# Extra rows multiplied four weight blocks at a time, their activation behind the two halves, and other steps for slots and turns in a mixture-of-experts block

## The chip, the cores and the metric

The kernel runs on one core of a Trainium2 chip, as one program. The metric is the device time of one execution in microseconds (us), the median of several runs. Besides the times there is one profiled execution, with the start and the duration of each engine's instructions and DMA packets.

## The reference

A block of an encoder over 1024 tokens of width 1024: a layer norm, two mixers (RWKV-7 and forgetting attention), an output projection, a layer norm, an expert layer with the top 4 of 32 experts, and a last layer norm. The change lies in the expert layer and in the last norm.

```
def _moe(h, router_w, router_b, w1, b1, w2, b2):
    logits = (xt @ router_w + router_b).astype(jnp.float32)
    top_val, top_idx = lax.top_k(logits, TOP_K)
    gates = jax.nn.softmax(top_val, axis=-1)
    ...
    def expert_block(args):
        xb, e = args
        hid = xb @ w1[e] + b1[e]
        x_glu = jnp.minimum(hid[..., ::2], SWIGLU_LIMIT)
        x_lin = jnp.clip(hid[..., 1::2], -SWIGLU_LIMIT, SWIGLU_LIMIT)
        act = x_glu * jax.nn.sigmoid(SWIGLU_ALPHA * x_glu) * (x_lin + 1)
        return act @ w2[e] + b2[e]
    ...
h = _layer_norm(x, ln_in_w, ln_in_b)
...
h = _layer_norm(DEEPNORM_ALPHA * h + mix, ln1_w[l], ln1_b[l])
ffn = _moe(h, ...)
h = _layer_norm(DEEPNORM_ALPHA * h + ffn, ln2_w[l], ln2_b[l])
```

## The kernel before

The first 1036 us (norms, mixers, projection, routing) are the same program in both kernels. Then the 32 experts run one after the other, in the order of the list `SEQ`, each with 128 rows ("main" rows); the 18 fullest ones have 32 rows more (the extras). In the order of the program the experts 4 to 28 form five periods of five: extras, extras, none, extras, none. So in each period one expert with extras follows another: 4 and 5, 9 and 10, 14 and 15, 19 and 20, 24 and 25. Expert 31, the last, has none.

**Weights.** An expert has twelve weight blocks of 1 MB, eight for `up` and four for `down`. SP loads each into one of six buffers `raw` (L1178). ScalarE rounds it to `wh` (the cast, L1185), VectorE takes the rest, `wl = raw - wh` (L1188). Both have four buffers, so a cast waits until TensorE has finished the block four places back. `weights(j, ahead)` calls these three blocks ahead of TensorE.

**Matmuls.** A block's main rows take twelve matmuls of 512 columns (xh with wh, xh with wl, xl with wh): in `up` into the PSUM tile `h` (L1213), in `down` into `o` (L1271). The extras are multiplied in fp32 straight from `raw`, into a PSUM tile `ex` of which there is one buffer, shared by `up` (L1206) and `down` (L1261). Their stationary side is 32 wide, and the trace has eight of them for a block. TensorE runs up(0), up(1), down(0), up(2), down(1) and so on: `down(r-1)` follows `up(r)`.

**Activation.** `act` gives the pieces of the swiglu (L1223 to L1227): `extra` reads `ex` of `up(r)` and writes `lx` (on VectorE gx, lx, lx, lx, with a sigmoid sx on ScalarE); `half(0)` and `half(1)` read two banks each of `h` and write `lm`. The `turns` transpose `lm` (tile `tr`, L1150), round it to `ah` on ScalarE (L1152) and take `al` on VectorE (L1153); the last turn transposes `lx` to `ax` (L1248). The bank `tr` has one buffer too.

**Steps.** Jobs run after each block: step 0 to 7 after the blocks of `up(r)`, 8 to 11 after those of `down(r-1)`. `plan(r, where, f)` puts a job there; XP and TP hold the steps of the pieces of the next expert's inputs and of the turns, SLP that of the slots. The slots work finds the rows of a coming expert: small matmuls (L1014, L1020), a copy `st` and `sv` to `gate` on VectorE (L1029, L1004 to L1010), and, for one with extras, a second small matmul from `st` (L1026). Each engine runs its own instructions in the order of the program.

After expert 31 its turns and the transposes of the one-hot matrix (L1401) come, then `down(31)`, then `final_norm`: eight sums of 128 tokens on TensorE (L1466, L1469), the statistics on VectorE, an inverse root by Newton steps in `chain` (L1478 to L1487), which `advance` runs one step at a time between other work, and scaling on ScalarE (L1496), GpSimd (L1497) and VectorE.

Of the kernel before, what the change touches and what calls it, by code (L numbers as in the profile page):

```python
# [18 lines left out]
P = 128  # L19
# [25 lines left out]
XP = (4, 5, 7)  # L45
TP = (11, 13, 14)
SLP = -4
# [7 lines left out]
XB = 2  # L55
# [1058 lines left out]
def experts(tc, A, L):  # L1114
# [3 lines left out]
    with ExitStack() as cx:  # L1118
# [55 lines left out]
        def weights(j, ahead):  # L1174

            while len(raws) < min(j + src[1], len(stream)):
                raw = wr.tile([P, 2 * FF], FT, name="raw", tag=src[0], bufs=src[2])
                sp.dma_start(raw, stream[len(raws)]())  # L1178
                raws.append(raw)
            while len(ready) < min(j + 1 + ahead, len(stream)):  # L1180
                i = len(ready)
                raw = raws[i]
                if i == len(highs):
                    highs.append(wr.tile([P, 2 * FF], FR, name="wh", bufs=WB))
                    ac.copy(highs[i], raw)  # L1185
                h = highs[i]
                l = wp.tile([P, 2 * FF], FR, name="wl", bufs=WB)
                ve.tensor_tensor(l, raw, f32(h), op=OP.subtract)  # L1188
                ready.append((raw, h, l))
            return ready[j]  # L1190

        def up(j0, sel, xh, xl, xt, step=lambda s: None):
# [6 lines left out]
            def extra(k, raw):  # L1199
                if px is None:  # L1200
                    return
# [6 lines left out]
            late = []  # L1208
            for k in range(KD):
                raw, h, l = weights(j0 + k, AH[xt is not None] if src[0] == "raw" else 0)  # L1210
                for x, w, z in ((xh, h, False), (xh, l, False), (xl, h, k == KD - 1)):
                    for c, m in enumerate(cols):
                        pe.matmul(ps[:, c], x[:, k], w[:, m], start=False, stop=z)  # L1213
                late.append((k, raw))
                if len(late) == XB:
                    for b in late:
                        extra(*b)
                    late.clear()
                step(k)
# [9 lines left out]
        def act(ps, px):  # L1229
# [20 lines left out]
            return [extra, lambda: half(0), lambda: half(1)], turns + [piece], (ah, al, ax)  # L1250

        def down(j0, ah, al, ax, gate, idx, step=lambda s: None, o=None):
# [3 lines left out]
            def extra(b, raw):  # L1256
                for c in range(2 if px is not None else 0):
# [5 lines left out]
            late = []  # L1263
            for b in range(4):
                raw, h, l = weights(j0 + b, AH[ax is not None] if src[0] == "raw" else 0)
# [6 lines left out]
                late.append((b, raw))  # L1272
                if len(late) == XB:
                    for x in late:
                        extra(*x)
                    late.clear()
# [62 lines left out]

        at = {}  # L1340
# [7 lines left out]
        with tc.manual_schedule():  # L1348
# [11 lines left out]
            for r in range(NE):  # L1360
# [18 lines left out]
                run_all(parts[:-2])  # L1379
                for i in range(2):  # L1380
                    jobs.setdefault(12 * r + DP + i, []).insert(0, parts[i - 2])
                for w, f in zip(TP, turns):
# [11 lines left out]

            ring = lambda: wr.tile([P, 2 * FF], FT, name="raw", bufs=RB)
            kept = ring()
            oht = kept[:, :S].rearrange("p (t q) -> p t q", t=NT)
            for g in range(2):
                ps = pq.tile([P, 4, P], FT, name="tr")
                for j in range(4):  # L1400
                    pe.matmul(ps[:, j], last_oh[0][:, 4 * g + j], idb, start=True, stop=True)  # L1401
                ac.copy(oht[:, 4 * g:4 * g + 4], ps)
# [8 lines left out]
            sums()  # L1411
            down(at["d", NE - 1], *prev, o=kept[:, S:])
# [37 lines left out]
def final_norm(tc, A, L, ep, pt, wb, ys, oht, o):  # L1450
# [51 lines left out]
    def advance(to_end=False):  # L1502
        nonlocal run
        while run is not None:
# [3 lines left out]
            if not to_end:  # L1508
                return

    for g0, g1 in zip(FG, FG[1:]):
# [9 lines left out]
        advance(True)  # L1521
# [5 lines left out]
    advance(True)  # L1527
# [58 lines left out]
```

## Time and profile before

| | |
|---|---|
| runs | 2580.55, 2583.0, 2586.46 us; median 2583.0 |
| profiled execution | 2580.89 us, of which its span 2579.2 |
| busy share of the span | TensorE 93%, VectorE 75%, ScalarE 51%, GpSimd 16% |
| before the experts | 0 to 1035.6 us |
| experts | 1035.6 to about 2530 us |
| final norm | 2531.8 to 2579.2 us |

Busy times are shares over a stretch; matmul records overlap, so that the distance of two starts says what a matmul costs. In brackets stands how long an engine sat idle before an instruction, and what ended it.

### The profile page before, as it was taken

To read this page: it belongs to the slowest core of one execution; us is meant where nothing else is said; L and a number is where in the kernel's file an instruction comes from. 1 tells how busy PE (TensorE), PEld (TensorE's weight loads), DVE (VectorE), ACT (ScalarE), POOL (GpSimd) and SP (SyncE) were. 2 spreads that over 40 slices of the span, in tenths; PEclk is the share of its full clock that TensorE was granted. 3 is DMA by queue.
4 is the path that set the end of the run, shared out by engine and by line. 5 is a ranking of instruction groups with operands and counts; after the bars stand their busy time and mean duration, and the time that the engine had idled before them with its cause. 6 is when DMAs were issued, how large, how long until landed. Compare 5 with 4: busy or idle time off the path is not lost. (4 is left out here: it accounts for less than half of the span.)

```text
span 2579.2 us, 37473 instructions
## 1 busy us (share of the span) xinstructions
PE 2399.2 (93%) x14105; PEld 1808.3 (70%) x14105; DVE 1928.0 (75%) x2886; ACT 1321.3 (51%) x1610; POOL 400.6 (16%) x370
## 2 busy tenths in 40 slices
PE   5999998989988996899999999999999999999986
PEld 5778998977776674657666666766676666667663
DVE  8367334376887687779788888888888888888884
ACT  3254432354344432456666656666565655666661
POOL 4400211123122011011101011011110110111012
PEclk9999999999999997899999999999999999999998
DMA  6323864228446424768878778888877897788973
GB/s 228 130 74 136 284 203 86 69 70 259 158 150 242 138 83 180 258 206 308 299 301 322 274 294 301 311 292 322 297 282 284 312 330 282 277 298 306 344 279 136
DMA packets 184442, 606.63 MB, mean 235 GB/s; under 512 B 69881, under 2 KB 95609, under 8 KB 130626
## 3 DMA queue, kind: packets, MB, share of 16 engines
q1 hardware_dynamic: 155810, 525.24, 55.0%
q0 software_dynamic: 17456, 65.02, 8.9%
q10 hardware_dynamic: 10992, 13.93, 1.8%
q8 instruction: 113, 1.85, 0.3%
q14 instruction: 71, 0.58, 0.1%
HBM read 518.64 MB, written 85.50 MB: 234 GB/s over the span
## 5 line engine op out<-in xcount | busy, mean ns | idle before, releaser
L1188 DVE TENSOR_TENSOR wl<-raw,wh 128x2048 fp32r<-128x2048 f32 x384 | 873.8, 2289 | 195.2 <-ACT wh L1185 194.1
L1185 ACT CAST wh<-raw 128x2048 fp32r<-128x2048 f32 x381 | 720.6, 1906 | 110.6 <-DMA raw<-w 83.4
L1213 PE MATMUL h<-wh,xh 128*128 128x512 f32 x1024 | 299.6, 414 | 0.9 <-ACT wh L1185 0.9
L1213 PE MATMUL h<-wl,xh 128*128 128x512 f32 x1024 | 281.3, 396 | 1.1 <-DVE wl L1188 1.1
L1213 PE MATMUL h<-wh,xl 128*128 128x512 f32 x1024 | 280.3, 395 | 0.0
L1213 PEld LDWEIGHTS h<-wl,xh 128*128 128x128 f32 x1024 | 193.2, 189 | 48.2 <-DVE wl L1188 1.6
L1213 PEld LDWEIGHTS h<-wh,xl 128*128 128x128 f32 x1024 | 192.4, 188 | 46.6
L1213 PEld LDWEIGHTS h<-wh,xh 128*128 128x128 f32 x1024 | 184.3, 190 | 52.9 <-ACT wh L1185 10.6
L1009 POOL DMA_INDIRECT xg<-h_d,idx x32 | 71.6, 2239 | 924.0 <-PE slots L1026 469.5
L153 PE MATMUL mm<-whi,hT_lo 128*128 128x256 f32 x640 | 187.1, 293 | 10.9 <-DVE hT_lo L182 7.3
L151 PE MATMUL mm<-whi,hT_hi 128*128 128x256 f32 x640 | 187.4, 294 | 6.0 <-ACT sq L476 4.3
L152 PE MATMUL mm<-wlo,hT_hi 128*128 128x256 f32 x640 | 186.1, 292 | 0.0
L1271 PE MATMUL o<-wh,ah 128*128 128x512 f32 x512 | 173.3, 420 | 0.0
L1271 PE MATMUL o<-wl,ah 128*128 128x512 f32 x512 | 164.9, 404 | 0.0
L1271 PE MATMUL o<-wh,al 128*128 128x512 f32 x512 | 164.0, 402 | 0.0
L1224 ACT ACTIVATE sm<-gm 128x512 f32<-128x512 f32 x64 | 40.4, 632 | 211.9 <-DVE gm L1223 211.9
L1206 PE MATMUL ex<-raw,xt 128*32 128x512 f32 x1152 | 139.7, 603 | 0.0
L153 PEld LDWEIGHTS mm<-whi,hT_lo 128*128 128x128 f32 x640 | 126.9, 199 | 12.9 <-DVE hT_lo L182 8.5
L151 PEld LDWEIGHTS mm<-whi,hT_hi 128*128 128x128 f32 x640 | 126.9, 198 | 9.3 <-ACT sq L476 4.7
L152 PEld LDWEIGHTS mm<-wlo,hT_hi 128*128 128x128 f32 x640 | 126.9, 198 | 0.0
L1271 PEld LDWEIGHTS o<-wh,ah 128*128 128x128 f32 x512 | 92.1, 193 | 34.8 <-issue 15.1
L1271 PEld LDWEIGHTS o<-wl,ah 128*128 128x128 f32 x512 | 98.8, 193 | 24.1
(432 smaller groups left out, 4177.7 us busy)
## 6 DMA issues: line engine op xcount, KB each, us to landing
raw<-w SPq DMA_DIRECT2D x384, 1024.0 KB
pks<-pk_d SPq DMA_DIRECT2D x16, 1152.0 KB
pk_d<-pk POOLq DMA_DIRECT2D x16, 896.0 KB, 5.6
h_d<-h SPq DMA_DIRECT2D x17, 512.0 KB
raw<-w_fx ACTq DMA_DIRECT2D x8, 1024.0 KB
fx_d<-fraw POOLq DMA_DIRECT2D x64, 128.0 KB, 2.6
qkvo<-fx_d SPq DMA_DIRECT2D x32, 256.0 KB
x<-x SPq DMA_DIRECT2D x8, 512.0 KB
```

The costliest lines, as they stand in the source:

```text
L151: pe.matmul(ps, hi[:, k, n], whi[:, k], start=(k == 0), stop=False)
L152: pe.matmul(ps, hi[:, k, n], wlo[:, k], start=False, stop=False)
L153: pe.matmul(ps, lo[:, k, n], whi[:, k], start=False, stop=(k == KD - 1))
L1009: gp.indirect_dma_start(out=x, out_offset=None, in_=h1_d, in_offset=bass.IndirectOffsetOnAxis(ap=idx[0:m, i:i + 1], axis=0))
L1185: ac.copy(highs[i], raw)
L1188: ve.tensor_tensor(l, raw, f32(h), op=OP.subtract)
L1206: pe.matmul(px[32 * c:32 * c + 32], xt[:, k], raw[:, m], start=False, stop=(k == KD - 1))
L1213: pe.matmul(ps[:, c], x[:, k], w[:, m], start=False, stop=z)
L1224: ac.activation(sg, g, AF.Sigmoid, scale=SWI)
L1271: pe.matmul(po[:, c], x[:, k], w[:, m], start=(k == 0 and x is ah and w is h), stop=z)
```

## The change

- The extras of `up` are multiplied after block 1 (for the blocks 0 to 3) and block 5 (4 to 7); before, after blocks 1, 3, 5 and 7 for two blocks each. In `down` all four come after block 1; before, after 1 and 3.
- `act` hands out its pieces as half(0), half(1), extra. `half(0)` runs at step 8 and `half(1)` at step 9 as before; `extra`, which ran ahead of step 8, is now planned for step 9 (DP + 1) and stands there behind `half(1)`.
- The slots move from step 8 to step 7, an expert's third input piece from step 7 to 6, the turn of `lx` from step 14 to 15 (after block 3 of the next `up`).
- Expert 31's halves run at once, its turns at steps 10 and 11, and the one-hot transposes at steps 8 and 9, all within `down(30)`.
- `advance()` in the final norm runs two steps of the chain a call.

```
-XP = (4, 5, 7)
-TP = (11, 13, 14)
-SLP = -4
+XP = (4, 5, 6)
+TP = (11, 13, 15)
+SLP = -5
...
-XB = 2
+XB = 4
+XM = 1
...
-                late.append((k, raw))
-                if len(late) == XB:
-                    for b in late:
-                        extra(*b)
-                    late.clear()
+                if px is not None and k % XB == XM:
+                    for b in range(k - XM, k - XM + XB):
+                        extra(b)
                 step(k)
...
-            return [extra, lambda: half(0), lambda: half(1)], turns + [piece], (ah, al, ax)
+            return [lambda: half(0), lambda: half(1), extra], turns + [piece], (ah, al, ax)
...
+                if px is not None and b == XM:
+                    for x in range(XB):
+                        extra(x)
                 step(KD + b)
...
                 parts, turns, a = act(*hid)
-                run_all(parts[:-2])
-                for i in range(2):
-                    jobs.setdefault(12 * r + DP + i, []).insert(0, parts[i - 2])
-                for w, f in zip(TP, turns):
+                if r < NE - 1:
+                    for i in range(2):
+                        jobs.setdefault(12 * r + DP + i, []).insert(0, parts[i])
+                    for f in parts[2:]:
+                        plan(r, DP + 1, f)
+                else:
+                    run_all(parts)
+                    for g in range(2):
+                        plan(r, KD + g, lambda g=g: turn_oh(g))
+                for w, f in zip(TP if r < NE - 1 else (10, 11), turns):
                     plan(r, w, f)
...
-    def advance(to_end=False):
+    def advance(n=2):
         while run is not None:
             if next(run[0], run) is run:
...
-            if not to_end:
+            n -= 1
+            if n == 0:
                 return
```

**What stands in VectorE's row at expert 5's activation.** Before: from the `wl` of block 2 of `down(4)` on; `ex_12138` is the PSUM tile that `up(5)` wrote.

```order
L1188 TENSOR_TENSOR wl_12330<-raw_12271,wh_12328 128x2048 [waits DMAHW2_49,Activation_49]
L1223 TENSOR_SCALAR gx_12357<-ex_12138 128x256 [waits PE_49]
L1225 TENSOR_SCALAR lx_12358<-ex_12138 128x256
L1226 SCALAR_TENSOR_TENSOR lx_12358<-lx_12358,gx_12357 128x256 [waits DVE_49]
L1227 TENSOR_TENSOR lx_12358<-lx_12358,sx_12359 128x256 [waits DVE_49,Activation_49]
L1188 TENSOR_TENSOR wl_12372<-raw_12304,wh_12370 128x2048 [waits DMAHW3_49,Activation_49]
L1223 TENSOR_SCALAR gm_12352<-h_12137 128x512
L1225 TENSOR_SCALAR lm_12353<-h_12137 128x512
L1226 SCALAR_TENSOR_TENSOR lm_12353<-lm_12353,gm_12352 128x512 [waits DVE_49]
L1227 TENSOR_TENSOR lm_12353<-lm_12353,sm_12354 128x512 [waits DVE_49,Activation_49]
L1029 COPY st_12412<-slots_12393 6x128 [waits PE_49]
```

In the changed kernel the same `wl` is followed by the slots' copies, the `wl` of block 3 and `half(0)`; the piece shown goes on from there, with the `wl` of block 0 of `up(6)`, `half(1)`, and then the extras.

```order
L1011 TENSOR_REDUCE gate_12352<-sv_12423 128x1
L1192 TENSOR_TENSOR wl_12436<-raw_12334,wh_12434 128x2048 [waits DMAHW4_49,Activation_49]
L1223 TENSOR_SCALAR gm_12387<-h_12137 128x512
L1225 TENSOR_SCALAR lm_12388<-h_12137 128x512
L1226 SCALAR_TENSOR_TENSOR lm_12388<-lm_12388,gm_12387 128x512 [waits DVE_49]
L1227 TENSOR_TENSOR lm_12388<-lm_12388,sm_12389 128x512 [waits DVE_49,Activation_49]
L1223 TENSOR_SCALAR gx_12392<-ex_12138 128x256
L1225 TENSOR_SCALAR lx_12393<-ex_12138 128x256
L1226 SCALAR_TENSOR_TENSOR lx_12393<-lx_12393,gx_12392 128x256 [waits DVE_49]
L1227 TENSOR_TENSOR lx_12393<-lx_12393,sx_12394 128x256 [waits DVE_49,Activation_49]
L1192 TENSOR_TENSOR wl_12480<-raw_12398,wh_12478 128x2048 [waits DMAHW5_49,Activation_49]
```

The read of `ex_12138` (gx, and lx behind it) moved from the second place behind that `wl` to a place behind two more `wl`, both halves and the slots' copies, and ahead of the `wl` of block 1 of `up(6)`.

**What stands in TensorE's row at the same place.** Before, from block 1 of `down(4)`; `ex_12367` is the tile that its extras fill, in the one buffer of `ex`.

```order
L1271 MATMUL o_12366<-wl_12308,ah_11999 128x512 x2
L1271 MATMUL o_12366<-wh_12306,al_12000 128x512 x2
L1261 MATMUL ex_12367<-raw_12220,ax_12004 32x512 [waits DMAHW0_49,DVE_49,PE_49]
L1261 MATMUL ex_12367<-raw_12220,ax_12004 32x512 x3
L1261 MATMUL ex_12367<-raw_12246,ax_12004 32x512 [waits DMAHW1_49]
L1261 MATMUL ex_12367<-raw_12246,ax_12004 32x512 x3
L1026 MATMUL slots_12452<-ident_82,st_12412 128x6 [waits DVE_49,PE_49]
L1271 MATMUL o_12366<-wh_12328,ah_11999 128x512 [waits Activation_49]
L1271 MATMUL o_12366<-wh_12328,ah_11999 128x512
```

The changed kernel, from the same matmuls of block 1:

```order
L1271 MATMUL o_12396<-wl_12316,ah_12022 128x512 x2
L1271 MATMUL o_12396<-wh_12314,al_12023 128x512 x2
L1262 MATMUL ex_12397<-raw_12224,ax_12027 32x512 [waits DMAHW0_49,DVE_49]
L1262 MATMUL ex_12397<-raw_12224,ax_12027 32x512 x3
L1262 MATMUL ex_12397<-raw_12246,ax_12027 32x512 [waits DMAHW1_49]
L1262 MATMUL ex_12397<-raw_12246,ax_12027 32x512 x3
L1262 MATMUL ex_12397<-raw_12271,ax_12027 32x512 [waits DMAHW2_49]
L1262 MATMUL ex_12397<-raw_12271,ax_12027 32x512 x3
L1262 MATMUL ex_12397<-raw_12312,ax_12027 32x512 [waits DMAHW3_49]
L1262 MATMUL ex_12397<-raw_12312,ax_12027 32x512 x3
L1271 MATMUL o_12396<-wh_12336,ah_12022 128x512 [waits Activation_49]
L1271 MATMUL o_12396<-wh_12336,ah_12022 128x512
```

The first matmul of `ex` waits for VectorE in both, for the second instruction that reads `up(5)`'s tile (the `lx` of L1225); all four blocks' extras now stand here in one run, and the main matmuls of blocks 2 and 3 stand behind them. The slots' matmul (L1026) has moved one block ahead.

**What stands in TensorE's row ahead of the last `down`.** Before, behind block 3 of `down(30)` (the four turns' matmuls follow one another; weight loads are rows of their own):

```order
L1271 MATMUL o_21821<-wh_21824,al_21541 128x512 x2
L1150 MATMUL tr_21902<-ident_82,lm_21817 128x128 [waits DVE_49,PE_49]
L1150 MATMUL tr_21902<-ident_82,lm_21817 128x128 x3
L1150 MATMUL tr_21912<-ident_82,lm_21817 128x128 [waits DVE_49]
L1150 MATMUL tr_21912<-ident_82,lm_21817 128x128 x3
L1401 LDWEIGHTS oh_21203
L1401 MATMUL tr_21920<-idb_10276,oh_21203 128x128 [waits DVE_49]
```

The changed kernel, at the end of block 1 of `down(30)` and into block 2:

```order
L1271 MATMUL o_21831<-wh_21782,al_21541 128x512 x2
L1345 LDWEIGHTS oh_21211
L1345 MATMUL tr_21877<-idb_10276,oh_21211 128x128 [waits Activation_49]
L1345 LDWEIGHTS oh_21211
L1345 MATMUL tr_21877<-idb_10276,oh_21211 128x128
L1345 LDWEIGHTS oh_21211
L1345 MATMUL tr_21877<-idb_10276,oh_21211 128x128
L1345 LDWEIGHTS oh_21211
L1345 MATMUL tr_21877<-idb_10276,oh_21211 128x128
L1271 MATMUL o_21831<-wh_21800,ah_21540 128x512 x2
L1271 MATMUL o_21831<-wl_21802,ah_21540 128x512 [waits DVE_49]
```

The one-hot transposes (now L1345) and, behind blocks 2 and 3, the turns of `lm` stand between the blocks of `down(30)`; before, all of them stood behind its last block.

## Rows read from the trace of the kernel before

**Rows 1.** The view of named stretches (start:end in us, its length; then for PE, PEld, DVE, ACT and POOL the busy us and the instruction count; the granted clock of TensorE as a share of full speed; the mean busy share of the DMA engines; GB/s): the whole expert stage, then one period of five experts in it.

```profile
1035.60:2530.00 1494.40, 1440.93 (x7639) 1004.79 (x7638) 1237.45 (x1184) 904.04 (x728) 179.60 (x97) 0.98 0.80 295
1286.50:1517.50 231.00, 225.75 (x1225) 156.18 (x1222) 194.93 (x187) 142.27 (x116) 28.12 (x16) 1.00 0.81 300
```

**Rows 2.** The groups of instructions by line and form in the expert stage (busy us, mean ns of one, idle before and what ended it): the weights' differences, the weights' casts, and the extras of `up` and of `down`.

```profile
L1188 DVE TENSOR_TENSOR wl<-raw,wh 128x2048 fp32r<-128x2048 f32 x383 | 871.5, 2289 | 195.2 <-ACT wh L1185 194.1
...
L1185 ACT CAST wh<-raw 128x2048 fp32r<-128x2048 f32 x381 | 720.6, 1906 | 110.6 <-DMA raw<-w 83.4 <-PE h L1213 18.2 <-issue 4.5
...
L1206 PE MATMUL ex<-raw,xt 128*32 128x512 f32 x1152 | 139.7, 603 | 0.0
L1261 PE MATMUL ex<-raw,ax 128*32 128x512 f32 x576 | 69.3, 598 | 0.0
```

**Rows 3.** What TensorE waited for in the expert stage (us in total, times, the longest).

```profile
PE slots L1026 <- DVE sv L1004: 25.8, 12, 6.1
PE tr L1248 <- DVE al L1153: 11.0, 7, 1.8
...
PE ex L1204 <- DVE ox L1292: 4.2, 1, 4.2
```

**Rows 4.** TensorE in order of time around expert 4's `down` with expert 5's `up` ending ahead of it (start us, us from the first start to the last end of a merged group, engine, line, operation, tile, count).

```profile
1299.11 1.10 PE L1213 MATMUL h<-wl,xh 128*128 128x512 f32 x4
1300.04 1.10 PE L1213 MATMUL h<-wh,xl 128*128 128x512 f32 x4
1301.07 1.92 PE L1206 MATMUL ex<-raw,xt 128*32 128x512 f32 x16
1302.92 0.73 PE L1271 MATMUL o<-wh,ah 128*128 128x512 f32 x2
1303.49 0.63 PE L1271 MATMUL o<-wl,ah 128*128 128x512 f32 x2
...
1305.83 0.35 PE L1014 MATMUL slots<-pv,oh 128*128 128x6 bf16 x8
...
1306.40 0.73 PE L1271 MATMUL o<-wh,ah 128*128 128x512 f32 x2
...
1309.40 1.92 PE L1261 MATMUL ex<-raw,ax 128*32 128x512 f32 x16
1311.93 0.35 PE L1026 MATMUL slots<-ident,st 6*128 6x6 f32 x2 [0.61 <-DVE sv L1004]
1312.22 0.74 PE L1271 MATMUL o<-wh,ah 128*128 128x512 f32 x2
```

**Rows 5.** The tile view of `ex` for the stretch of its first group in rows 4 (count, ns of one, start of the first and of the last).

```profile
L1206 PE MATMUL ex<-raw,xt x16: 592/592/617, 1301.1 to 1302.4; 128*32 128x512 f32 x16
```

**Rows 6.** VectorE in order of time over the same piece.

```profile
1301.61 2.29 DVE L1188 TENSOR_TENSOR wl<-raw,wh 128x2048 fp32r<-128x2048 f32 x1
1303.82 0.42 DVE L1223 TENSOR_SCALAR gx<-ex 128x256 f32<-128x256 f32 x1
1304.15 0.42 DVE L1225 TENSOR_SCALAR lx<-ex 128x256 f32<-128x256 f32 x1
...
1308.72 0.68 DVE L1223 TENSOR_SCALAR gm<-h 128x512 f32<-128x512 f32 x1
...
1311.44 0.27 DVE L1029 COPY st<-slots 6x128 f32<-6x128 f32 x1
...
1312.29 2.28 DVE L1188 TENSOR_TENSOR wl<-raw,wh 128x2048 fp32r<-128x2048 f32 x1
1314.49 0.16 DVE L1004 COPY sv<-slots 128x6 f32<-128x6 f32 x1
...
1315.15 0.68 DVE L1223 TENSOR_SCALAR gm<-h 128x512 f32<-128x512 f32 x1
...
1318.33 4.49 DVE L1188 TENSOR_TENSOR wl<-raw,wh 128x2048 fp32r<-128x2048 f32 x2 [0.38 <-ACT wh L1185]
```

**Rows 7.** ScalarE in order of time, the same piece: the extras' sigmoid.

```profile
1304.27 0.42 ACT L1224 ACTIVATE sx<-gx 128x256 f32<-128x256 f32 x1 [3.42 <-DVE gx L1223]
```

**Rows 8.** The view of stretches again: after the 4.2 us wait of rows 3 (first row), after the slots' wait in expert 12's and in expert 27's stretch, the first and the last of four such (next two), and at the turn ahead of the last `down` (last row).

```profile
1135.00:1142.00 7.00, 5.52 (x26) 2.26 (x26) 5.14 (x3) 4.75 (x4) 1.55 (x2) 0.51 0.87 228
1637.00:1640.30 3.30, 3.30 (x9) 2.55 (x8) 3.23 (x8) 0.21 (x1) 2.68 (x2) 0.50 1.06 400
2333.20:2336.50 3.30, 3.30 (x10) 2.53 (x9) 3.23 (x8) 0.27 (x1) 2.74 (x2) 0.51 1.01 390
2510.70:2521.00 10.30, 7.23 (x24) 5.72 (x25) 3.93 (x4) 4.51 (x5) 1.77 (x1) 0.50 0.61 139
```

**Rows 9.** TensorE in order of time at the end of the expert stage, from the end of expert 31's `up`.

```profile
2493.62 0.63 PE L1271 MATMUL o<-wh,ah 128*128 128x512 f32 x2
...
2511.70 1.11 PE L1150 MATMUL tr<-ident,lm 128*128 128x128 f32 x4 [6.28 <-DVE al L1153]
...
2515.81 1.20 PE L1271 MATMUL o<-wh,ah 128*128 128x512 f32 x2
...
2531.76 0.70 PE L1466 MATMUL y<-raw,ident 128*128 128x512 f32 x1 [2.17 <-ACTq L1417]
```

**Rows 10.** ScalarE and GpSimd in order of time at the end of the final norm.

```profile
2563.03 3.23 ACT L1496 ACTIVATE raw<-raw,frr 128x1024 f32<-128x1024 f32 x3 [5.62 <-DVE frr L1487]
...
2564.26 6.96 POOL L1497 TENSOR_TENSOR raw<-raw 128x1024 f32<-128x1024 f32 x3 [1.86 <-ACT raw L1496]
```

More of the change, by code (lines that the diff above doesn't have):

```diff
@@ L1172, in experts, with load @@
         src = ["raw", RB, RB]
-        def weights(j, ahead):
-            while len(raws) < min(j + src[1], len(stream)):
+        def load(n):
+            while len(raws) < min(n, len(stream)):
                 raw = wr.tile([P, 2 * FF], FT, name="raw", tag=src[0], bufs=src[2])
@@ L1179, in weights @@
                 raws.append(raw)
+        def weights(j, ahead):
+            load(j + src[1])
             while len(ready) < min(j + 1 + ahead, len(stream)):
@@ L1197, in up, with extra @@
                 pe.matmul(ps[:, c], sel, bh[:, m], start=True, stop=False)
-            def extra(k, raw):
-                if px is None:
-                    return
+            def extra(k):
+                raw = raws[j0 + k]
                 if k == 0:
@@ L1206, in extra @@
                     pe.matmul(px[32 * c:32 * c + 32], xt[:, k], raw[:, m], start=False, stop=(k == KD - 1))
-            late = []
             for k in range(KD):
-                raw, h, l = weights(j0 + k, AH[xt is not None] if src[0] == "raw" else 0)
+                _, h, l = weights(j0 + k, AH[xt is not None] if src[0] == "raw" else 0)
                 for x, w, z in ((xh, h, False), (xh, l, False), (xl, h, k == KD - 1)):
@@ L1254, in down, with extra @@
             px = pq.tile([P, 512], FT, name="ex") if ax is not None else None
-            def extra(b, raw):
-                for c in range(2 if px is not None else 0):
+            def extra(b):
+                raw = raws[j0 + b]
+                for c in range(2):
                     for kk in range(2):
@@ L1261, in extra @@
                         pe.matmul(px[32 * g:32 * g + 32], ax[:, kk, 32 * b:32 * b + 32], raw[:, m], start=(b == 0), stop=(b == 3))
-            late = []
             for b in range(4):
-                raw, h, l = weights(j0 + b, AH[ax is not None] if src[0] == "raw" else 0)
+                _, h, l = weights(j0 + b, AH[ax is not None] if src[0] == "raw" else 0)
                 for kk in range(2):
@@ L1271, in down @@
                             pe.matmul(po[:, c], x[:, k], w[:, m], start=(k == 0 and x is ah and w is h), stop=z)
[L1272 to L1276, printed above, removed]
+                if px is not None and b == XM:
+                    for x in range(XB):
+                        extra(x)
                 step(KD + b)
@@ L1338, in step, with turn_oh @@
                 f()
+        ring = lambda: wr.tile([P, 2 * FF], FT, name="raw", bufs=RB)
+        kept = []
+        def turn_oh(g):
+            ps = pq.tile([P, 4, P], FT, name="tr")
+            for j in range(4):
+                pe.matmul(ps[:, j], last_oh[0][:, 4 * g + j], idb, start=True, stop=True)
+            if g == 0:
+                load(len(stream))
+                kept.append(ring())
+            ac.copy(kept[0][:, :S].rearrange("p (t q) -> p t q", t=NT)[:, 4 * g:4 * g + 4], ps)
         at = {}
@@ L1393, in experts @@
                 step(NE, s)
[L1395 to L1402, printed above, removed]
             wb = ring().rearrange("p (i d) -> p i d", i=2)
@@ L1411, in experts @@
             sums()
+            kept = kept[0]
+            oht = kept[:, :S].rearrange("p (t q) -> p t q", t=NT)
             down(at["d", NE - 1], *prev, o=kept[:, S:])
@@ L1520, in final_norm @@
             advance()
-        advance(True)
+        advance(0)
         run = (chain(g0, g1), g0, g1)
@@ L1526, in final_norm @@
         pe.matmul(bp[0][:, c], L["ons"][0:1], wb[0:1, 1, 512 * c:512 * c + 512], start=True, stop=True)
-    advance(True)
+    advance(0)
 def L_lor(lor, which):
```

## The prediction

> **What bounds the kernel now.** I read the stretches first: all edits lie in the expert stage or behind it, and of its 1494 us TensorE is busy 1441, in a period of five experts 226 of 231 [rows 1]. VectorE is busy 195 of 231 there, ScalarE 142. So work taken from TensorE's row is time, work moved off VectorE is none by itself, but VectorE, 84% busy and in order, decides where TensorE stands still. The waits come next: TensorE waits 25.8 us for the slots' copies in 12 places, 11.0 us in 7 places at the transposes of `lx`, once 4.2 us at `ex` [rows 3]. Then one expert's `down` on both engines gives the distances with which the new order can be walked through [rows 4, 6].
>
> **The change part by part.**
>
> *Longer runs of extras.* A group of 16 extras matmuls costs more than its 16: the last main group before it is 1.03 us from it where groups are otherwise 0.93 apart; the first pair behind it takes 0.57 instead of 0.47 [rows 4]; and from the group's start to the next main matmul are 1.85 us, while its four passes start 0.43 apart (three of them from 1301.1 to 1302.4) and so need 1.72 [rows 5], 0.13 more. That is 0.33 us a group where main matmuls follow, and at least 0.10 (the entry alone) where something else does. The 1152 and 576 matmuls [rows 2] are 72 groups in `up` and 36 in `down`, 18 experts with four and two; they become two and one. 54 groups go. I take 0.27 for each, between the bounds and near the upper, since most are followed by main matmuls: **-14.5 us** (-5 to -18).
>
> *The extras' activation behind the halves.* This decides the case, and it is the wait in TensorE's row shown with the change. In five places `up(r)` and `down(r-1)` both have extras and share the one buffer `ex`. TensorE may begin the extras of `down(r-1)` only when gx and lx of `up(r)` have been read. Before, these stood ahead of both halves and were done at 1304.57, long before TensorE came there at 1309.40 [rows 4, 6]: the wait was hidden by two blocks of `down`. Now, with T0 as the end of block 7's main matmuls (1300.97 in these rows):
> TensorE arrives at T0 + 0.57 (slots, 1305.83 to 1306.40) + 2.91 (block 0, 1302.92 to 1305.83) + 0.29 (slots' second matmul) + 2.90 (block 1) = T0 + 6.7 [rows 4].
> VectorE begins the `wl` of `down`'s block 2 at T0 + 0.64 (1301.61). Then: `wl` 2.21, slots' copies 0.85 (1311.44 to 1312.29), `wl` 2.21, half 2.72 (1308.72 to 1311.44), second copies 0.66 (1314.49 to 1315.15), `wl` 2.20, half 2.80 (1315.15 to 1318.33 less 0.38 idle), gx and lx 0.75 [rows 6]. Sum 14.4, so T0 + 15.0.
> TensorE stands still for **8.3 us**, five times: **+41.5**. What it has queued behind the wait are blocks 2 and 3 of `down` and the next expert, all main work. The lower bound is 7.0: the cast of block 2 can't begin before block 6 is done, 2.8 us ahead of T0, and takes 1.91 [rows 2], so that `wl` can't begin before T0 - 0.7 with some 0.2 for the release. The upper bound is 9: a cast that comes behind a sigmoid adds its 0.4 to 0.6.
>
> Can the main matmuls behind the wait go ahead of it? At 1311.93 TensorE sat idle 0.61 us with `o` matmuls behind the one that waited, and they came after it [rows 4]. If they could, 5.7 us of blocks 2 and 3 would pass, and 2.6 of each 8.3 would remain, 13 in all. [...]
>
> *The clock after it.* [...] A stretch of t us at half clock loses t/2: 5.5 busy us lose 2.75, 7.2 lose up to 3.6, 3.3 lose 1.65. [...]
>
> *Waits that go.* Of the 12 slots' waits one is 6.1 and five are like the 0.61 of rows 4; the other six share 16.7, some 2.5 to 2.8 each [rows 3]. Five of them are in the periods' fourth experts, where the copies stand behind a half; now slots and copies stand ahead of it. 5 x 2.5, with the four half-clock stretches behind them 4 x 1.65: -19. The transposes of `lx` wait up to 1.8 us for `al` in the third expert [rows 3]; a block later, with VectorE caught up: -9. The 0.61 in the second [rows 4]: -2.5. Together **-30.5** (-15 if the copies, still behind a `wl`, keep half of it; -35).
>
> *Waits that come in the other experts with extras.* In the first and fourth of a period `down(r-1)` has no extras, so nothing blocks at once, but gx to lx (1.73 us in all) and the sigmoid sx now stand ahead of the work for block 1 of the next `up`. gx begins at T0 + 14.2, sx 0.45 later for 0.42 [rows 6, 7]; the cast of that block stands behind sx and needs 1.91, then `wl` 2.21: ready at T0 + 19.1 to 19.3. TensorE needs that `wl` at T0 + 6.7 + 5.8 (two blocks) + 0.5 (transposes) + 0.7 + 2.8 (bias and block 0) + 0.9 = T0 + 17.4. I take 1.5 in the first kind; in the fourth, where the transposes of `lm` then also wait for `al` (the wait of 1.4 to 1.8 that rows 3 has in the next `up`), 3: 5 x 4.5 = **+22.5** (0 if VectorE comes earlier, as it may behind the 8.3 us pause; 30 if both wait 3).
>
> *Experts 0 to 3, 29 and 30.* Slots a block earlier against their waits there, some 9 of the 25.8 us: the copies are still queued behind `wl`, I take **-2.5** (-8 to +3).
>
> *The last expert.* T0 is 2493.62; `down(31)` begins 22.2 us later, after waits of 6.28 and more, and at half clock until 2521 [rows 8, 9]. With the halves at once and the turns inside `down(30)`: four blocks 11.2, four transpose groups 1.6, then waits: for ScalarE's copy of the first one-hot group behind both sigmoids and a cast (2), for `al` between the turns (1), for ScalarE's scaling of `o`, one buffer, behind `ah` (2.5). Start at T0 + 18.3, and block 0 without the half clock: 4 + 2.4, of which the loads of the sums, which wait for the scattered result of expert 30, may keep some: -6. The chain in the final norm: ScalarE waits 5.62 us for it until 2563.03, and GpSimd's three passes follow until 2571 [rows 10]; two steps per call end it before the last sums: -2. Together **-8** (-3 to -12).
>
> **Sum:** -14.5 + 41.5 + 12.5 - 30.5 + 22.5 - 2.5 - 8 = +21. On the profiled 2580.9 this is 2602. The median of the runs is 2583.0, 2.1 above the profiled execution; where the waits overlap (a pause gives VectorE time that the next wait is short of) the sum is a little high. I say **2602** for the median, +19. A measurement here can tell about 0.2%, 5 us.
>
> **The rivals.**
>
> 1. *VectorE catches up in the pause, faster.* The 8.3 us stand, but VectorE goes on through them; if it stays a block ahead after them, the 22.5 of the other experts don't come and the clock is back within one matmul block. Then -14.5 + 41.5 - 30.5 - 2.5 - 8 = -14: 2569. It speaks for it that VectorE has 36 us free of 231; against it that its delays come from casts that can't start before TensorE frees a buffer (194 of the 195 us idle ahead of `wl` end with a cast [rows 2]), so it can't work ahead of TensorE by more than four blocks. It decides where clock and new waits together stay under 9 of their 35 us (under 14 it is no change). The main matmuls that pass the wait would end here too: -14 - 28 = -42, 2541, 0.01 of the chance, since the idle row speaks against it. Chance 0.12.
> 2. *No change.* The pause costs the lower bound 7.0 (35), the clock half (6), the new waits 11: -3.5 in all, or with slightly more +4. Chance 0.11.
> 3. *Slower, as forecast*, by 6 to 33 us: 0.70.
> 4. *Much slower.* Half clock for as long as in the last turn (3.6 each, +5.5), waits of 3 in both kinds (+7.5), and four `raw` buffers that come free at once behind each pause, so that the following loads arrive late, say 1 us a time in 18 experts: 2602 + 31 = 2633. The DMA engines' share is 0.81 in a period [rows 1], with a pause of 8 us they have slack, which speaks against. Chance 0.07.
>
> **How the numbers follow.** Faster is rival 1, 0.12; same 0.11; slower 0.70 + 0.07 = 0.77. The likeliest case lies between 2589 and 2616. The range has to leave out no more than 0.2: below 2582 lie rival 1 and a small part of the no-change case, some 0.14, above 2616 some 0.06. That is 2582 to 2616.
>
> **What would show it.** In the changed kernel's trace the wait list of TensorE should have `ex` (L1262) waiting for VectorE's lx five times, 7 to 9 us each, in all about 40, and no such wait elsewhere; half clock behind each; the slots' waits down from 25.8 to about 10; those at L1248 gone; new waits of 1 to 3 us at block 1 of `up` behind experts 4, 7, 9, 12 and so on. The extras should stand in groups of 32, two to an `up` and one to a `down`. `down(31)` should start 18 us after T0 at full clock. It is wrong if the `ex` waits are under 5 us (then VectorE stood earlier than I walk it), or if the periods are shorter than 231 us in spite of them.

## Result

The changed kernel takes 2608.95 us (median; 2603.04 to 2614.49) against 2581.78 us before: the ratio is 1.0098, with a 95% interval of 1.008 to 1.0116. It is 27 us slower. The forecast was 2602, slower, within 2582 to 2616. The total came out right by luck, as the experiments show: the longer groups, put down as a gain, are a loss, the gain put for the end did not come, and the terms of the new order together are three times too large.

The profiled execution is 2612.61 us (span 2610.9), 31.7 above the one of before. Worked out from the starts of each expert's bias matmuls in the two timelines, 2.5 us of this lie ahead of the experts (in a program that is the same, so they come from the runs), 1.9 in experts 0 to 3, 26.2 in the five periods, -0.8 in experts 29 and 30, and 1.8 from there to the end.

What TensorE waited for in the experts, changed kernel (us in total, times, longest), to be read against [rows 3]:

```profile
PE ex L1262 <- DVE lx L1225: 36.4, 5, 7.3
PE h L1215 <- DVE wl L1192: 12.4, 13, 1.1
PE slots L1015 <- DVE oh L1140: 7.6, 13, 0.6
PE tr L1151 <- DVE al L1154: 6.3, 8, 1.6
...
PE slots L1027 <- DVE sv L1005: 1.9, 1, 1.9
```

The forecast wait is there, at `ex`, five times and nowhere else, 7.3 us each. The 25.8 us at the slots are 1.9, the transposes of `lx` are gone from the list. New are 13 short waits for `wl` and 13 of 0.6 us at the slots' first matmuls, for the one-hot rows `oh`.

The place itself, TensorE and then VectorE around the end of expert 5's `up`, answers [rows 4, 6]:

```profile
1306.85 1.09 PE L1215 MATMUL h<-wh,xl 128*128 128x512 f32 x4
1308.55 0.36 PE L1015 MATMUL slots<-pv,oh 128*128 128x6 bf16 x8 [0.60 <-DVE oh L1140]
...
1322.77 4.93 PE L1262 MATMUL ex<-raw,ax 128*32 128x512 f32 x32 [7.27 <-DVE lx L1225]
...
1333.77 1.03 PE L1201 MATMUL h<-bh,sel 96*128 96x512 bf16 x4
```

```profile
1308.41 2.28 DVE L1192 TENSOR_TENSOR wl<-raw,wh 128x2048 fp32r<-128x2048 f32 x1
...
1317.04 2.28 DVE L1192 TENSOR_TENSOR wl<-raw,wh 128x2048 fp32r<-128x2048 f32 x1
1319.24 0.69 DVE L1223 TENSOR_SCALAR gm<-h 128x512 f32<-128x512 f32 x1
...
1322.30 0.41 DVE L1225 TENSOR_SCALAR lx<-ex 128x256 f32<-128x256 f32 x1
```

T0, the end of the main matmuls of `up`, is 1307.78. VectorE begins the `wl` at T0 + 0.63 and has read `ex` with lx at 1322.71, T0 + 14.9; the walk gave T0 + 15.0. TensorE came there at 1322.77 - 7.27 = T0 + 7.7, 1.0 later than walked; 0.60 of that is the slots' wait for `oh`. So the wait is 7.3 and not 8.3.

TensorE's clock behind two of the five waits (columns as in [rows 1]):

```profile
1318.60:1325.40 6.80, 2.63 (x16) 0.67 (x20) 5.58 (x10) 2.83 (x3) 1.49 (x1) 0.50 0.46 176
1554.10:1564.30 10.20, 5.44 (x28) 1.39 (x32) 7.71 (x10) 2.83 (x3) 2.09 (x1) 0.50 0.56 192
```

It is at 0.50 for 6.8 or 10.2 us, also while TensorE waits (until 1322.77 in the first); of these it is busy 2.6 and 5.4, in all five 21.2 us; half of that, 10.6 us, is lost, an estimate from these busy times and the clock. The forecast had 12.5.

### The profile page after: what moved, and what is told of

The parts are those of the page before. It is cut to its first block, busy times and chain, and to the rows that moved or that the text cites. A ratio compares the mean times of both kernels' runs of the same rounds, so it can differ in the third digit from the quotient of the medians.

```text
span 2610.9 us, 37454 instructions
## 1 busy us (share of the span) xinstructions
PE 2397.8 (92%) x14105; PEld 1813.1 (69%) x14105; DVE 1925.0 (74%) x2886; ACT 1319.1 (51%) x1610; POOL 435.1 (17%) x370
## 3 DMA queue, kind: packets, MB, share of 16 engines
q8 instruction: 113, 1.85, 0.3%
## 5 line engine op out<-in xcount | busy, mean ns | idle before, releaser
L1189 ACT CAST wh<-raw 128x2048 fp32r<-128x2048 f32 x381 | 720.2, 1906 | 114.5 <-PE h L1215 45.6
L1215 PE MATMUL h<-wl,xh 128*128 128x512 f32 x1024 | 284.3, 400 | 12.4 <-DVE wl L1192 12.4
L1215 PEld LDWEIGHTS h<-wl,xh 128*128 128x128 f32 x1024 | 193.3, 190 | 64.0 <-DVE wl L1192 18.3
L154 PE MATMUL mm<-whi,hT_lo 128*128 128x256 f32 x640 | 187.5, 294 | 10.6 <-DVE hT_lo L183 7.7
L154 PEld LDWEIGHTS mm<-whi,hT_lo 128*128 128x128 f32 x640 | 127.2, 199 | 12.5 <-DVE hT_lo L183 8.9
L1209 PE MATMUL ex<-raw,xt 128*32 128x512 f32 x1152 | 132.2, 600 | 0.0
L1282 POOL DMA_INDIRECT ya_d<-o,idx x31 | 60.6, 1956 | 406.7 <-ACT o L1279 406.7
```

Source lines behind the costliest of these rows:

```text
L154: pe.matmul(ps, lo[:, k, n], whi[:, k], start=False, stop=(k == KD - 1))
L1209: pe.matmul(px[32 * c:32 * c + 32], xt[:, k], raw[:, m], start=False, stop=(k == KD - 1))
L1282: gp.indirect_dma_start(out=ya_d, out_offset=bass.IndirectOffsetOnAxis(ap=idx[:, 0:1], axis=0), in_=o, in_offset=None, compute_op=OP.add)
```

## Experiments

The ratios stand against the kernel before, run on the same chip in the same batch; its median there is given beside. A "period" gives the lengths of its five experts (extras, extras, none, extras, none), from one expert's bias matmuls to the next's in the timeline, as means over the five periods (four for the fifth expert), and their sum. Before: 45.4, 50.5, 43.6, 49.8, 42.4, together 231.6. Changed: 44.9, 60.7, 41.3, 45.8, 44.2, together 236.9.

### The activation back in its place

```
-            return [lambda: half(0), lambda: half(1), extra], turns + [piece], ...
+            return [extra, lambda: half(0), lambda: half(1)], turns + [piece], ...
...
-                    for f in parts[2:]:
-                        plan(r, DP + 1, f)
+                    run_all(parts[:-2])
```

> The changed kernel with one part undone: the extras' activation stands ahead of half(0) again, everything else as changed. Theory (the wait at ex and its clock are the loss): no wait of TensorE at ex for lx; the second expert of a period falls from about 60.7 us to about 49.5, the waits for wl at block 1 behind the other experts go too; 2535 to 2555 us, faster than before, since the longer groups and the slots' step are then left as gains. Rival (the longer groups free four raw buffers at once and starve the loads, or the slots' and turns' steps cost): it stays at 2580 or above.

2587.81 us against 2583.34, ratio 1.0018 (1.0003 to 1.0033). The wait at `ex` and the long second expert are gone (47.2, 50.4, 43.5, 47.7, 43.5, together 232.2), and yet the rest of the change is no gain. TensorE waits elsewhere:

```profile
PE h L1201 <- DVE lm L1225: 24.0, 13, 2.3
PE slots L1015 <- DVE oh L1140: 7.6, 13, 0.6
```

The first row is the bias matmuls of the next expert, which wait for `half(1)`. So the wait at `ex` is a loss of this change, and not the only one: the expected 2535 to 2555 supposed that the groups of four are a gain.

### The new order and steps without the groups of four

The kernel before with the order of the changed one in `act` and the new XP, TP and SLP.

> The kernel before with the extras' activation behind half(1) and the new steps of slots, third piece and lx turn; extras still in groups of two blocks, end and final norm as before. Theory: five waits at ex of 7 to 8 us as in the changed kernel, half clock behind them; about 2609 + 12 (the 54 groups that come back) - 2 = 2615 to 2622 us. Rival (the wait needs the groups of four): waits under 3 us, under 2590 us.

2588.35 against 2583.34, ratio 1.0015 (1.0003 to 1.0028); period 45.5, 58.1, 41.6, 45.6, 43.4, together 234.1.

```profile
PE ex L1261 <- DVE lx L1225: 30.7, 5, 6.3
```

The wait needs no groups of four: it is there with 6.1 us on average, TensorE coming 1.2 us later to it, since it has the last two blocks' extras to do first. But the total is 20 us less than in the changed kernel, and that is the part of the groups, the end and the norm. Expected were 2615 to 2622.

### The groups of four alone

```
-XB = 2
+XB = 4
+XM = 1
```

> The kernel before with the extras in groups of four blocks and nothing else. Theory: 54 groups at 0.27 us fewer, -14.5 us, 2567 (-5 to -18). Rival: TensorE comes earlier to the same VectorE waits (slots, lx turn) and gives it back there: those waits grow by as much, 2578 to 2582.

2626.69 against 2583.34, ratio 1.0147 (1.012 to 1.0174): 38 us slower, where the prediction put -14.5. Period 46.6, 49.8, 47.4, 51.9, 42.0, together 237.6.

```profile
PE slots L1027 <- DVE sv L1005: 38.9, 12, 7.2
PE tr L1245 <- DVE al L1154: 19.8, 6, 3.8
PE h L1198 <- DVE lm L1222: 10.5, 7, 2.3
```

The slots' waits grew from 25.8 to 38.9 us and those at `lx` from 11.0 to 19.8 [rows 3], and 10.5 are new. In the fourth expert the slots wait 4.51 instead of 2.47 us, at `lx` in the third it is 3.81 instead of 1.80: each about 2.0 more, near the 1.85 us of one group of extras [rows 4]. The rival of the expectation, that the waits take the gain back, was on the right way and far too small.

### The activation between the halves

```
-                    for f in parts[2:]:
-                        plan(r, DP + 1, f)
+                    for f in parts[2:]:
+                        jobs.setdefault(12 * r + DP, []).insert(1, f)
```

> The changed kernel with the extras' activation between half(0) and half(1) (step 8) in place of behind half(1). Theory: VectorE reads ex one wl, one half and some copies earlier, 5 to 5.7 us; the five waits fall from 7.3 to 1.5 to 2.5 us each, 10 us in all, and TensorE's clock mostly holds; 2560 to 2575 us. Rival (the wait is set by something else than VectorE's row ahead of it, a load or a cast): the waits stay over 5 us.

2570.65 against 2583.34, ratio 0.9941 (0.9921 to 0.9962), period 46.7, 51.5, 41.3, 47.0, 42.8.

```profile
PE h L1201 <- DVE lm L1225: 17.2, 13, 1.8
PE ex L1262 <- DVE lx L1225: 8.4, 5, 1.7
```

One `wl`, one half and the copies less ahead of the read, and the wait falls from 7.3 to 1.7 us, 5.6 less, as worked out from VectorE's rows. That the row of VectorE ahead of the read sets the wait is shown by this.

### Only the reads between the halves

gx, lx and the sigmoid between the halves, the two instructions that don't read `ex` behind `half(1)`.

> The changed kernel with the two reads of ex (gx, lx) and their sigmoid between half(0) and half(1), and the two instructions that only need gx and lx behind half(1). Theory (what matters is when ex and h are read, not when the extras' activation is done): the wait at ex stays at 1.5 to 1.8 us as with the whole activation between the halves, and the 13 waits of the next expert's bias matmuls for lm (17.2 us there) fall by 0.8 us each: 2560 to 2567 us. Rival (the rest of the activation now holds up the next wl as much): 2569 to 2573.

2580.71 against 2585.61, ratio 0.9981 (0.9967 to 0.9995): slower than with the whole activation between (0.9941), and the intervals lie apart. The bias matmuls wait 17.9 us as before (17.2), because the `wl` between the halves doesn't begin earlier:

```profile
1645.38 0.42 DVE L1245 TENSOR_SCALAR lx<-ex 128x256 f32<-128x256 f32 x1
1647.75 2.29 DVE L1192 TENSOR_TENSOR wl<-raw,wh 128x2048 fp32r<-128x2048 f32 x1 [1.29 <-ACT wh L1189]
```

```profile
1645.50 0.42 ACT L1244 ACTIVATE sx<-gx 128x256 f32<-128x256 f32 x1 [1.82 <-DVE gx L1243]
1645.83 1.89 ACT L1189 CAST wh<-raw 128x2048 fp32r<-128x2048 f32 x1
```

Its cast stands behind the sigmoid on ScalarE and takes 1.89 us; the 0.9 us that VectorE saved became idle time (1.29 us, where it was 0.30 with the whole activation between). Neither theory had that. Why it is slower by some 10 us stays open: the waits at `lm`, `ex` and `al` are only 2.3 us longer in all (17.9, 8.5 and 4.6 against 17.2, 8.4 and 3.1).

### The extras of down behind block 3

```
-                if px is not None and b == XM:
+                if px is not None and b == 3:
```

> The changed kernel with the extras of down all behind block 3 in place of block 1. Theory (the wait at ex ends when VectorE reads lx, 14.9 us behind the end of up, whatever TensorE has done by then): TensorE does blocks 2 and 3, 5.7 us, first, and the five waits fall from 7.3 to 1.6 us or less, with little half clock: 2570 to 2582 us. Rival (the buffers raw, held two blocks longer, make the next loads late): new waits for casts behind the experts with extras, 2595 and more.

2620.92 against 2585.61, ratio 1.014 (1.0117 to 1.0164). The five waits fell as expected, and the time rose:

```profile
PE ex L1207 <- DVE ox L1290: 31.9, 12, 4.6
PE ex L1262 <- DVE lx L1225: 8.4, 5, 1.7
```

The tile `ex` has one buffer, and done two blocks later it is read two blocks later, by ox (L1290); now the extras of the next `up` wait for that, 12 times, 2.7 us on average. The expected loss from late loads wasn't it; the wait moved to the buffer's next user.

### The end alone

The kernel before with expert 31's halves at once, its turns at steps 10 and 11 and the one-hot transposes at 8 and 9.

> The kernel before with only the end changed: expert 31's halves at once, its turns and the one-hot transposes inside down(30). Theory (the last norm starts when the four loads of the sums have landed, and they wait for the scattered result of expert 30, whose scaling on ScalarE comes later now): no gain, 0 to +3 us, though down(31) starts 3 to 4 us earlier. Forecast of the prediction: -6.

2589.79 against 2585.61, ratio 1.0022 (1.0008 to 1.0037). TensorE and SP at the end:

```profile
2515.00 1.22 PE L1274 MATMUL o<-wh,ah 128*128 128x512 f32 x2 [1.69 <-ACT o L1284]
...
2536.23 3.78 PE L1481 MATMUL y<-raw,ident 128*128 128x512 f32 x4 [8.33 <-SPq L1432]
```

```profile
2521.64 2.02 SPq L1423 DMA_DIRECT2D raw<-ya_d  x4
```

The last norm waits 8.33 us, for the loads of the sums, 14.6 us behind their issue. So `down(31)` begins 17.3 us behind the end of `up(31)`, where it was 22.2, and the first sum 38.6 us behind it, where it was 38.1 [rows 9]. The forecast gain of 6 isn't there.

### The groups behind the last blocks

The groups alone with XM = 3: groups of four behind blocks 3 and 7 of `up`, 3 of `down`.

> The kernel before with groups of four blocks of extras at blocks 3 and 7 of up and 3 of down, in place of 1 and 5, and 1. Theory (groups at 1 and 5 lost because TensorE came 1.9 us earlier to the waits behind up; behind block 7 the group covers them): the slots' waits fall below those of the kernel before, 2560 to 2575 us. Rival 1 (long groups are bad wherever they stand): 2610 and more. Rival 2 (the buffers are held longer and loads come late): waits for casts, 2585 and more.

2774.36 against 2585.61, ratio 1.0743 (1.072 to 1.0766). What ScalarE (from 1290 to 2500 us) and TensorE waited for most:

```profile
ACT wh L1186 <- DMA raw<-w: 252.0, 63, 10.9
```

```profile
PE tr L1151 <- DVE xl L1154: 77.9, 18, 5.7
PE slots L1027 <- DVE sv L1005: 63.1, 17, 8.4
```

The casts wait 252 us for the loads, where in the kernel before they wait 63.2 in the same stretch: the buffers `raw`, held two blocks longer, aren't free in time (a load waits up to 20.4 us for the extras of an `up` to be done with its buffer, where it was up to 9.2). It tells nothing on the cover that it was meant to tell.

### Steps, order and groups taken apart

Three kernels on one chip: the kernel before with the new XP, TP and SLP alone; with the activation between the halves too; and with that and the groups of four. The end and the last norm are as before.

> The kernel before with nothing but the new steps (slots, third piece, turn of lx). Theory (the slots' waits and the half clock behind them go, as the prediction has it): the 25.8 us of slots' waits fall under 6, the fourth expert of a period from 49.8 to about 46, 2562 to 2572 us. Rival (the waits move to the next place where TensorE needs VectorE, the bias matmuls of the next expert): these waits appear with 1 to 2 us each, 2578 us and more.

> The same with the extras in groups of two blocks, as before the change. Theory (a removed group is worth 0.28 us where TensorE's waits are short): 10 to 15 us slower than with groups of four, 2575 to 2583 us. Rival (TensorE, earlier by the groups' gain, waits it off again, as in groups_alone): 2560 to 2569, as fast or faster.

> The kernel before with the new steps, the extras' activation between the halves and the groups of four; end and final norm as before (so it is extras_between without the changed end). Theory (the changed end costs 3 to 4 us, as it did alone): 2564 to 2569 us, 0.6 to 0.8% faster than before. Rival (the end gains here): over 2571.

| kernel | us (before 2581.45) | ratio | period |
|---|---|---|---|
| steps alone | 2558.79 | 0.9914 (0.9898 to 0.9930) | 46.3, 49.8, 42.3, 46.3, 43.1: 227.8 |
| and between, groups of two | 2549.14 | 0.9872 (0.9852 to 0.9891) | 45.8, 50.5, 41.6, 45.9, 43.1: 226.8 |
| and groups of four | 2572.83 | 0.9959 (0.9947 to 0.9972) | 46.7, 51.5, 41.3, 47.0, 42.8: 229.4 |

The steps alone are a gain of 23 us, more than expected; the slots' waits are gone, as the prediction has it, and in their place are 6.2 us at the bias matmuls:

```profile
PE h L1197 <- DVE lm L1225: 6.2, 10, 0.8
```

The groups of four cost 24 us here, in the same order and steps, where a gain of 10 to 15 was expected. Where, the fourth expert of the second period shows. With groups of two, TensorE at the end of its `up` (the first row is the last main group) and at the next expert's bias matmuls, then ScalarE and VectorE from block 6 on:

```profile
1616.73 1.10 PE L1213 MATMUL h<-wh,xl 128*128 128x512 f32 x4
1617.76 1.92 PE L1206 MATMUL ex<-raw,xt 128*32 128x512 f32 x16
...
1632.53 1.02 PE L1197 MATMUL h<-bh,sel 96*128 96x512 bf16 x4
```

```profile
1612.27 0.59 ACT L1152 CAST xh<-tr 128x512 fp32r<-128x512 f32 x1 [2.77 <-PE tr L1150]
1612.76 1.91 ACT L1185 CAST wh<-raw 128x2048 fp32r<-128x2048 f32 x1
```

```profile
1614.70 2.29 DVE L1188 TENSOR_TENSOR wl<-raw,wh 128x2048 fp32r<-128x2048 f32 x1 [1.11 <-ACT wh L1185]
...
1618.31 2.28 DVE L1188 TENSOR_TENSOR wl<-raw,wh 128x2048 fp32r<-128x2048 f32 x1
```

With groups of four:

```profile
1629.28 1.10 PE L1212 MATMUL h<-wh,xl 128*128 128x512 f32 x4
1630.98 0.35 PE L1015 MATMUL slots<-pv,oh 128*128 128x6 bf16 x8 [0.60 <-DVE oh L1140]
...
1645.06 1.02 PE L1198 MATMUL h<-bh,sel 96*128 96x512 bf16 x4 [1.11 <-DVE lm L1222]
```

```profile
1627.23 2.29 DVE L1189 TENSOR_TENSOR wl<-raw,wh 128x2048 fp32r<-128x2048 f32 x1 [1.11 <-ACT wh L1186]
...
1630.84 2.28 DVE L1189 TENSOR_TENSOR wl<-raw,wh 128x2048 fp32r<-128x2048 f32 x1
```

From the last main group to the next expert's bias matmuls are 15.80 us in the one (1616.73 to 1632.53) and 15.78 in the other (1629.28 to 1645.06), though the second has no extras to do in that stretch. VectorE's last `wl` shown begins 1.58 us behind the last group's start in the one and 1.56 in the other, the `wl` ahead of it 2.03 and 2.05 us before that start. That one waits for its cast, which stands on ScalarE behind `xh`, the rounding of the transposes `tr` that TensorE makes between blocks 5 and 6 of `up`, behind the extras. So VectorE's row hangs on how far TensorE is in `up`; what TensorE does behind it fills time that it would wait anyway. The extras of blocks 6 and 7, moved ahead of those transposes, delay all of it by 1.4 us (their 1.7 less one group's 0.3; measured from this expert's bias matmuls to its last main group, 29.87 and 31.26 us), and the place that they left is idle: 0.60 and 1.11 us.

### Longer groups without leaving that place

```
-                late.append((k, raw))
-                if len(late) == XB:
-                    for b in late:
-                        extra(*b)
-                    late.clear()
+                if px is not None and k in (1, 5, 7):
+                    for b in {1: range(4), 5: (4, 5), 7: (6, 7)}[k]:
+                        extra(b, raws[j0 + b])
```

> The kernel between_groups_of_two with one change: in up the extras of blocks 0 to 3 in one group behind block 1, those of 4 and 5 behind block 5, those of 6 and 7 behind block 7, in down groups of two as before the change. Theory (a longer group costs only because it takes the 1.9 us of extras away from behind block 7, where they give VectorE the time that TensorE waits off otherwise): 18 groups at 0.28 us fewer, and no new wait for slots, ex or lm; 2541 to 2549 us. Rival (any group of four costs, by the order in which buffers come free): 2555 and more.

2549.85 against 2584.45, ratio 0.9863 (0.9842 to 0.9883). Period 45.5, 50.2, 41.6, 45.5, 43.1, together 225.7: each expert with extras is about 0.3 us shorter than with groups of two, where the clock is the same (third period: 45.79 and 45.48, 50.38 and 50.11, 45.66 and 45.34), the others are the same. The waits hold still (2.8 and 1.7 us with groups of two):

```profile
PE ex L1258 <- DVE lx L1222: 2.9, 5, 0.8
PE h L1197 <- DVE lm L1222: 1.0, 2, 0.6
```

So a group that is saved is worth 0.3 us where the group behind block 7 stays, and the loss of the groups of four is the leaving of that place. `down` has its groups of two again here, but its group of four is no rival: in the table's last two kernels the stretch from the last main group to the next bias matmuls in a period's third expert, with the extras of `down` in it and none of `up`, is 16.9 us with groups of two and 16.6 with groups of four. In the median of the runs these 5 us can't be told from nothing (0.9863 and 0.9872 overlap). The two are the fastest kernels here, 32 to 35 us under the one before and 59 under the changed one.

## Why the prediction was right, and where not

- **The wait at `ex`**: right in place, count and reason. 5 x 7.3 = 36.4 where 41.5 stood; the 1.0 us of each is TensorE's later arrival, 0.6 of it the wait for `oh`, which the walk left out. The main matmuls of blocks 2 and 3 stayed behind it, as the prediction took from the row of the 0.61 us idle [rows 4]: at expert 5 the first of them starts at 1327.62, behind the extras that waited until 1322.77.
- **The clock**: right; 10.6 us lost (the estimate from the trace) where 12.5 stood. The 12.5 was the author's estimate, 2.5 for each of five waits, and no run shows that figure; the busy times of 5.5, 7.2 and 3.3 us beside it are those of [rows 8], at 0.51 and 0.50. What the runs showed in its place is 0.50 for 6.8 us at three of the waits and for 10.2 at two, with TensorE busy for 2.6 to 6.0 us of it.
- **Waits that go**: right in which go, the gain a third smaller. The steps alone give -23 where -30.5, with the half clock, and -2.5 for the experts 0 to 3, 29 and 30 stood; 6 us come back at the bias matmuls.
- **Waits that come in the other experts (+22.5)**: put down to one edit, where it takes two. With the new order and groups of two the list has none but the one of before (1.1 us); the first, third and fourth expert are 0.7 to 0.8 us shorter than with the steps alone, the fifth 0.3 longer, and the bias matmuls' waits for `lm` fall from 6.2 to 0.7 us, since the halves come 1.7 us earlier. The waits for `wl` come with the groups of four, 12.4 us in the changed kernel, at the place forecast (the `up` behind the first and fourth expert). The order's whole cost, from 0.9914 to 1.0015 of before, is 26 us, where 41.5 + 12.5 + 22.5 = 76.5 stood for it: the five second experts take 41 where 54 stood for wait and clock, and the others give 15 back where 22.5 more stood. What the halves gain for being earlier was left out of the sum.
- **Longer groups (-14.5)**: the step that failed. The price was right, 0.27 put and 0.3 measured, but the sum took work off TensorE as time, wherever it stood ("work taken from TensorE's row is time"). What the runs showed in its place: an `up` with extras takes 1.4 us more, since the work stands ahead of what VectorE's row hangs on, and where it stood before TensorE now waits. Alone the groups cost 38 us, in the new order with the activation between 24; in the changed kernel they, the end and the norm make up 21 us (1.0098 against 1.0015). There the first expert is even 0.6 us shorter than with groups of two, and the loss is in the second and fifth (2.6 and 0.8 longer), which have the 12.4 us of waits for `wl`.
- **The last expert (-8)**: wrong. `down(31)` starts at 2542.05, T0 + 18.5 (18.3 put), but not at full clock as forecast: it is 0.50 from 2540.6 to 2547.4, so that block 0 takes 5.3 us, as before (5.2). And the norm's first sums come at 2563.77, T0 + 40.3, where it was 38.1 before [rows 9]. The chain that sets them runs another way. Engine by engine (TensorE, ScalarE, SP) in the changed kernel, and then ScalarE and SP in the one before:

```profile
2542.05 1.22 PE L1271 MATMUL o<-wh,ah 128*128 128x512 f32 x2 [1.92 <-ACT o L1279]
...
2563.77 2.93 PE L1476 MATMUL y<-raw,ident 128*128 128x512 f32 x3 [7.84 <-SPq L1427]
```

```profile
2537.17 1.06 ACT L1467 ACTIVATE raw<-raw 128x1024 f32<-128x1024 f32 x1 [1.66 <-DMA raw<-ln_w]
...
2540.87 1.13 ACT L1279 ACTIVATE o<-o,gate 128x1024 f32<-128x1024 f32 x1
```

```profile
2533.27 0.34 SPq L1413 DMA_DIRECT2D raw<-ln_w  x1
...
2549.04 2.12 SPq L1418 DMA_DIRECT2D raw<-ya_d  x4
```

```profile
2508.70 1.12 ACT L1281 ACTIVATE o<-o,gate 128x1024 f32<-128x1024 f32 x1
```

```profile
2517.17 4.01 SPq L1410 DMA_DIRECT2D raw<-ya_d  x4
```

  ScalarE waits 1.66 us for the load of the norm's weights, which is issued later (T0 + 9.7, where it was T0 + 4.5) since VectorE frees its buffer behind both halves (SP waits 10.3 us for a `wl` behind them; before, it waited 5.0 us for a `wl`); so the scaling of expert 30's `o` is at 2540.87, T0 + 17.4, where it was T0 + 15.1. Its result is scattered (landed at 2548.98), the loads of the sums are issued from 2549.04 on, T0 + 25.5 where it was 23.6, and the first sum follows 14.7 us behind, as with the end alone (14.6): the last load has landed at 2563.04, and SP passes the branch of L1427, which the row of TensorE names, at 2563.26. The prediction named these loads as what "may keep some"; they kept all. The chain in the norm, two steps a call, shows no gain where 2 us were put: from its first sum to the end of the span are 47.1 us, where it was 47.4 before, and 47.2 to 48.1 in four other kernels that have it.
- **The rivals.** The faster one needed VectorE to catch up in the pause, with clock and new waits under 9 us together; they were 23 (10.6 and 12.4). That the total held was luck: 50 us too much for the order (76.5 against 26) met 43 too little for groups, end and norm (-22.5 against 21).

What stays open is what the end costs. Alone it is 1.0022, but with groups and between, 0.9941 with it (and the norm) and 0.9959 without it. The traces of that pair don't put this gain at the end: from the end of `up(31)` to the end of the span are 86.5 us with it and 85.6 without, the experts take equally long, and 4.3 us lie ahead of them, in a program that is the same. That last stretch is 85.6 us before, 87.4 in the changed kernel, 88.9 with the end alone; but it is 88.0 with the steps alone, whose end is the old one, so that single executions don't settle it.

That the groups alone cost 38 us and some 24 on the new steps is seen in the periods, 6.0 us longer against 2.6. The difference lies mostly in the third expert (3.8 longer against 0.3 shorter), where the new steps have no wait at `lx`. And the clock of the groups alone is at half behind each of the ten waits in the third and fourth experts of the periods, for 3.4 or 6.8 us, 54 us in all; in the later pair it is nowhere at half in the periods (mean granted clock of the executions 0.958, against 0.975 with groups of two and 0.973 with groups of four).

## What to carry to other kernels

Work on the busiest engine isn't all worth its time: what stands between the last instruction that another engine's row hangs on and the first result that must come back from that engine covers a wait, and moved ahead of that instruction it delays everything by its length (here the extras of blocks 6 and 7: 1.4 us more in `up`, and 0.60 and 1.11 us idle in their place). So before terms are summed, ask of each what the engine would do in its place. And a buffer with one copy passes a wait on (here `ex`: 12 waits, 31.9 us, at its next user): before a read or a write of it is put later, list who uses it next.

## What the runs showed of the hardware

The granted clock fell to half (0.50) in all five waits of 7.3 us, for 6.8 us in three and 10.2 in two of them, partly while TensorE still waited. So the same wait cost between 1.3 and 3.0 us more (an estimate, half of the 2.63 to 5.95 us that TensorE was busy at that clock), and the second expert's length went from 59.9 to 61.5 us in one execution. From the first expert's bias matmuls to the last one's the clock was at half for 20 us in the kernel with groups of 4, 2 and 2, for 38 before and for 185 with the groups behind the last blocks; the mean granted clock of these executions was 0.974, 0.972 and 0.946. So in these runs a change in waits counted for more than its own length.
